# Matmul order in a chunked gated recurrence: two heads in turn, state products after score products

## The chip, the cores and the metric

The kernel runs on one core of one Trainium2 chip. The metric is the device time of one execution in microseconds (us). The kernel before takes 2736.16 us as the median of three runs (2735.38, 2736.16 and 2738.37).

## What is computed

One layer of a hybrid decoder trunk over 2048 tokens of width 1024: a normalised input, one combined input projection, four causal token mixers side by side (A: RG-LRU, B: mLSTM, C: HGRN2, D: GLA), a projection per mixer, a gated merge, an output projection and a final norm. The change lies in the code that C and D share, the gated recurrence:

```python
def gla_chunkwise(q, k, v, log_g):                 # per head, in chunks
    def step(state, xs):
        qc, kc, vc, gc = xs
        G = jnp.cumsum(gc, axis=2)
        diff = jnp.where(mask, G_t - G_s, -jnp.inf)
        A = einsum('bhtd,bhsd,bhtsd->bhts', qc, kc, jnp.exp(diff))          # scores
        o = einsum('bhts,bhse->bhte', A, vc) + einsum('bhtd,bhde->bhte', qc * jnp.exp(G), state)
        state = jnp.exp(G_last) * state + einsum('bhsd,bhse->bhde', kc * jnp.exp(G_last - G), vc)
        return state, o
```

C has four heads with 128 key channels each, D has four heads with 64 key channels and 128 value channels each. Everything is float32.

## The kernel before

The 2048 tokens go through in two halves of 1024. In each half the input projection of most columns comes first (`ahead_pairs`), then `mixers` with the chunked recurrences, then `merge` (branch projections times gates, summed) and `outp`. Large projections take exact splits of their operands into two float32r parts (`proj_ch` L268, `tok_mm` L280, `ip_pair` L422); the recurrences multiply in plain float32, and each such product stands in the trace as two MATMUL records.

`mixers` goes through 12 steps of `gla_tile`, one step for 128 key channels and 512 tokens (4 chunks of 128). Steps 0 to 7 are mixer C: one head fills the 128 partitions, `heads` is `[(0, 128)]`. Steps 8 to 11 are mixer D: two heads share the partitions, `heads` is `[(0, 64), (64, 64)]`, so a product contracts over 64 partitions, those from 0 for one head and those from 64 for the other. There are four such two-head tiles in a half, eight in the program.

One call of `gla_tile` has these stages on TensorE:

- L985, in `diag`: the scores of blocks of 32 tokens on the diagonal, 16 products of 32x32 for a head, once for the inner blocks of 8 and once each for m = 8 and m = 16. A head writes a PSUM bank of its own, block b to partitions from 32 b.
- L1028: the blocks off the diagonal for m = 32 (8 products of 32x32 for a head) and m = 64 (4 products of 64x64 for a head).
- L1050: transposes of the decayed keys. L1056: the chunks' additions to the state, heads in turn. L1063 (VectorE) folds these into the states at the four chunk starts.
- L1071 and L1072: the outputs. L1071 multiplies a chunk's scores (`atv`, 128 partitions) by its values, L1072 the decayed queries (`eg`, the head's partitions alone) by the state, both summed in PSUM.
- L1094: transposes of the normalised outputs; L1095 (VectorE) multiplies them by the gate from the bank.

Six PSUM banks (`bank()`, tiles `mx`) go round among all recurrences; two more (`pb`) belong to the projections. The order on each engine is not written by hand: the framework's scheduler lays the instructions out from priorities and dependencies, and fills the recurrences' waits with projections (L268, L280). During steps 8 to 11 the filler is `merge`'s branch projections, L268. Each engine's instructions stand in that fixed order.

```python
    for c in range(4):
        for b in range(4):
            s0 = c * 128 + b * 32
            T.matmul(ps[b * 32:(b + 1) * 32, c * 32:(c + 1) * 32], wk[p0:p0 + K, s0:s0 + 32],
                     wq[p0:p0 + K, s0:s0 + 32], start=True, stop=True)
```

Of the kernel before, what the change touches and what calls it, by code (L numbers as in the profile page):

```python
# [12 lines left out]
ALU = mybir.AluOpType  # L13
# [4 lines left out]
HT = 1024  # tokens of a half  # L18
DM = 1024
KT = 8  # k tiles of d_model  # L20
U = 516  # columns of one arena unit
NU = 16  # arena units that stay
NA = 4  # tiles of two units that are the arena's outside of the fast products
NY = 8  # the same, and branch outputs in the merge
NP = 6  # merge gates (of 32) computed between the mixers
NE = 5  # of these, so many for the first tokens while the others are split
EPS = 1e-6
NPB = 2  # PSUM banks of the input projection; the other ones are the mixers'
NG = 10  # arena units of the fast products; the other ones are what follows them
PRE = (("mx", 4), ("mo", 4), ("mz", 4), ("hq", 4), ("hz", 4), ("gz", 4), ("gq", 2), ("gk", 2))  # paths to DRAM, with their tiles  # L30
# [12 lines left out]
NORM = {"hz": "hnw", "gz": "gnw"}  # gate paths with the norm's weight in them  # L43
SILU = ("lz", "mz", "hq", "hz", "gz")
FILL = [0, 2, 0, 0, 0, 1, 0, 0, 1, 0, 0, 0, 2, 0]  # merge gates projected before each stage of the mixers

# columns of the packed per-channel vectors
# [10 lines left out]
# channel-major column tiles of the input projection, in the order of wc  # L58
# [10 lines left out]
# constants that depend on shapes alone  # L69
# [29 lines left out]
class Arena:  # L99
    """Units of U columns, handed out in program order, round and round; pairs start at even units."""  # L100
# [47 lines left out]
class Trunk:  # L148
# [107 lines left out]
    def proj_ch(self, pieces, rh, rl, sink, ns=(0, 1)):  # L256
        """128 columns of a product for 512 tokens at a time from weight pieces of 4 k tiles
        each: sink(token slice, PSUM [128, 512])."""
        nc = self.nc
        nk = 4 * len(pieces)  # L260
        for n in ns:
            ts = slice(n * 512, (n + 1) * 512)
            ps = self.pbank()
# [18 lines left out]
    def ip_tok(self, pieces, ncol, evac, single=8):  # L282
        """Token-major column group: evac(first chunk, PSUM [128 tokens, chunks, ncol]); chunks one by one from some."""
# [10 lines left out]
    def ip_tok_k(self, pieces, evac, ks):  # L294
        """The same for 256 columns, k outermost: the operands' tiles are done with one by one."""
        vs = [p[:, 0:256].unsqueeze(1) for p in [self.pbank() for _ in range(NPB)] + [self.bank() for _ in range(8 - NPB)]]
        for k in ks:
            for c in range(8):
                self.tok_mm(vs[c][:, 0, :], c, k, pieces, 256, k == ks[0], k == ks[-1])
        for c in range(8):  # L300
            evac(c, vs[c])

# [6 lines left out]
    def split_first(self, xs):  # L309
        """The normalised input of the first tokens"""  # L310
# [7 lines left out]
    def load_first(self, xs):  # L318
        """The first tokens, and merge gates from them before the norm's factor is known"""
# [40 lines left out]
    def split_blocks(self, xs, st):  # L360
        """The other blocks (two of tokens by two of channels) that the products take: one more as it
        is, four sums; the block left out goes to DRAM."""
# [22 lines left out]
    def restore_block(self):  # L385
        """The block left out of the products, where its sum was."""
# [13 lines left out]
    def ip_pair(self, t0, t1, fin):  # L400
        """Two column tiles of 1024 tokens each; fin of both, [128, 3 free + 1024]."""
# [56 lines left out]
    def ahead_pairs(self):  # L458
        """The projections that the mixers take channel by channel, as far as no other channel or
        earlier token is needed, the RG-LRU, and merge gates: to DRAM."""  # L460
# [122 lines left out]
    def setup_mix(self):  # L583
        nc, c, a, col = self.nc, self.const, self.a, self.col
        V, A = nc.vector, nc.scalar
        # RG-LRU
# [8 lines left out]
        V.tensor_scalar(self.clru, self.clru, 4.0, None, op0=ALU.mult)  # 8 softplus(-lam) / 2  # L595
# [5 lines left out]
        # mLSTM: conv halved (for silu through tanh)  # L601
# [25 lines left out]
        # HGRN2 lower bound: cumulative softmax over the one layer, less its first  # L627
# [14 lines left out]
        # GLA  # L642
        nc.sync.dma_start(self.wlr, a["g_w_lr2"])

# [1 line left out]
    def load_h(self, half, xs, ns=(0, 1)):  # L646
        """The normalised input before it is split: 8 tiles of [128 channels, 1024 tokens]"""
# [41 lines left out]
    def carried(self, f, ci):  # L689
        """The last three tokens before a projection tile, in front of it."""  # L690
# [4 lines left out]
    def load_p(self, name, j, g):  # L695
        """512 tokens of a projection tile"""
# [4 lines left out]
    def conv(self, f, dst, w, b):  # L701
        """w: four per-channel taps, b: bias"""
# [6 lines left out]
    def lru(self, j, fx, zg, temp):  # L709
# [4 lines left out]
        r = [fx[:, h * 512:(h + 1) * 512] for h in range(2)]  # once the convolution is through  # L714
        w = xc
# [39 lines left out]
    def mconv(self, j, f, temp):  # L755
        """silu of the convolution, to DRAM"""
# [10 lines left out]
    def mlstm_rows(self, g, temp):  # L767
        """Gates of 512 tokens: column forms, and row forms in DRAM."""
# [54 lines left out]
    def mlstm(self):  # L823
        """The chunks of 128 tokens; yields where another mixer's work can come in between."""
# [23 lines left out]
        def scores(c, xm, mx, r1b, wib):  # L848
# [10 lines left out]
            # value rows, with a column of ones  # L859
# [681 lines left out]
```

## Time and profile before

| | |
|---|---|
| median of three runs | 2736.16 us (2735.38 to 2738.37) |
| profiled execution, first to last instruction (span) | 2737.5 us |
| time of the profiled execution itself | not listed apart from the span; the runs lie within 2.2 us of it |
| TensorE matmuls (PE) | busy 2603.8 us, 95% of the span, 16800 records |
| TensorE weight loads (PEld) | busy 2153.6 us, 79% |
| VectorE (DVE), ScalarE (ACT), GpSimd (POOL) | busy 1736.1, 1291.6, 1499.7 us |
| mean granted TensorE clock | 0.978 of full |

A record's duration covers its way through the array, and matmuls overlap, so what a matmul costs is read from start to start, not from its duration. The three float32 lines L985, L1028 and L1071/L1072 have small groups on the page; their cost shows in the timeline.

### The profile page before, as it was taken

To read this page: it belongs to the slowest core of one execution; us is meant where nothing else is said; L and a number is where in the kernel's file an instruction comes from. 1 tells how busy PE (TensorE), PEld (TensorE's weight loads), DVE (VectorE), ACT (ScalarE), POOL (GpSimd) and SP (SyncE) were. 2 spreads that over 40 slices of the span, in tenths; PEclk is the share of its full clock that TensorE was granted. 3 is DMA by queue.
4 is the path that set the end of the run, shared out by engine and by line. 5 is a ranking of instruction groups with operands and counts; after the bars stand their busy time and mean duration, and the time that the engine had idled before them with its cause. 6 is when DMAs were issued, how large, how long until landed. Compare 5 with 4: busy or idle time off the path is not lost. (4 is left out here: it accounts for less than half of the span.)

```text
span 2737.5 us, 45829 instructions
## 1 busy us (share of the span) xinstructions
PE 2603.8 (95%) x16800; PEld 2153.6 (79%) x16800; DVE 1736.1 (63%) x2907; ACT 1291.6 (47%) x2763; POOL 1499.7 (55%) x1273
## 2 busy tenths in 40 slices
PE   7889999999989898999999999999999999999999
PEld 5667788877878876778977777888787888777789
DVE  8987853346667767743478878533477677776332
ACT  5554554334444565542465545533344445644433
POOL 5556644444546545567476666444455556554753
PEclk9999999999999999999999999999999999989999
DMA  6132334243454435795442322433335533458821
GB/s 227 61 109 89 101 119 139 98 145 103 148 170 128 121 121 189 253 317 165 155 138 94 110 91 89 139 116 108 135 113 179 167 118 106 146 190 308 273 93 74
DMA packets 227072, 393.03 MB, mean 144 GB/s; under 512 B 20720, under 2 KB 78080, under 8 KB 226848
## 3 DMA queue, kind: packets, MB, share of 16 engines
q1 hardware_dynamic: 226848, 390.11, 42.7%
q8 instruction: 132, 2.16, 0.3%
q14 instruction: 92, 0.75, 0.1%
HBM read 270.42 MB, written 119.60 MB: 142 GB/s over the span
## 5 line engine op out<-in xcount | busy, mean ns | idle before, releaser
L417 POOL TENSOR_TENSOR wl<-wr,wh 128x512 fp32r<-128x512 f32 x264 | 371.6, 1411 | 302.4 <-ACT wh L416 294.4
L417 POOL TENSOR_TENSOR wl<-gth,wh 128x512 fp32r<-128x512 f32 x198 | 284.4, 1437 | 294.6 <-ACT wh L416 284.2
L422 PE MATMUL mx<-s,wh 128*128 128x512 f32 x1296 | 408.5, 395 | 11.3 <-DVE s L306 4.7
L431 DVE TENSOR_TENSOR arena<-arena,mx 128x512 f32<-128x512 f32 x348 | 229.4, 681 | 221.8 <-PE mx L422 208.5
L250 POOL TENSOR_TENSOR wl<-wr,wh 128x512 fp32r<-128x512 f32 (+1 forms) x176 | 250.4, 1431 | 175.4 <-ACT wh L249 139.8
L422 PE MATMUL mx<-hh,wh 128*128 128x512 f32 x760 | 302.0, 397 | 11.9 <-DVE arena L431 10.2
L422 PE MATMUL mx<-hh,wl 128*128 128x512 f32 x760 | 302.3, 398 | 3.1 <-POOL wl L417 3.1
L422 PE MATMUL mx<-hl,wh 128*128 128x512 f32 x760 | 302.0, 397 | 2.0 <-DVE hl L306 2.0
L422 PEld LDWEIGHTS mx<-s,wh 128*128 128x128 f32 x1296 | 243.9, 188 | 70.6 <-DVE s L306 7.1
L268 PE MATMUL pb<-hh,wh 128*128 128x512 f32 x704 | 286.9, 409 | 7.4 <-ACT hh L1284 2.6
L268 PE MATMUL pb<-hl,wh 128*128 128x512 f32 x704 | 286.5, 407 | 5.8 <-DVE hl L1285 5.8
L268 PE MATMUL pb<-hh,wl 128*128 128x512 f32 x704 | 284.3, 404 | 0.0
L416 ACT ACTIVATE wh<-wr 128x512 fp32r<-128x512 f32 x264 | 164.5, 627 | 232.7 <-PE mx L422 98.4
L280 PE MATMUL pb<-wh,hh 128*128 128x256 f32 (+1 forms) x880 | 254.2, 290 | 3.7 <-ACT arena L1006 1.5
L422 PE MATMUL mx<-s,wl 128*128 128x512 f32 x648 | 256.2, 396 | 0.9 <-POOL wl L417 0.9
L280 PE MATMUL pb<-wl,hh 128*128 128x256 f32 (+1 forms) x880 | 253.4, 288 | 1.7 <-POOL wl L250 1.7
L280 PE MATMUL pb<-wh,hl 128*128 128x256 f32 (+1 forms) x880 | 253.5, 288 | 0.0
L416 ACT ACTIVATE wh<-gth 128x512 fp32r<-128x512 f32 x198 | 124.4, 629 | 246.6 <-DVE gth L427 201.6
L249 ACT ACTIVATE wh<-wr 128x512 fp32r<-128x512 f32 (+1 forms) x176 | 110.0, 629 | 161.9 <-PE pb L268 106.6
L422 PEld LDWEIGHTS mx<-hh,wh 128*128 128x128 f32 x760 | 144.3, 190 | 50.1 <-ACT arena L218 11.0
L422 PEld LDWEIGHTS mx<-hh,wl 128*128 128x128 f32 x760 | 143.6, 189 | 41.0 <-POOL wl L417 8.2
L422 PEld LDWEIGHTS mx<-hl,wh 128*128 128x128 f32 x760 | 144.0, 189 | 38.1 <-DVE hl L306 3.2
(614 smaller groups left out, 6177.6 us busy)
## 6 DMA issues: line engine op xcount, KB each, us to landing
wr<-in_wc_dram SPq DMA_DIRECT2D x246, 256.0 KB, 2.7
g<-arena SPq DMA_DIRECT2D x52, 512.0 KB, 3.4
gth<-in_wc_dram SPq DMA_DIRECT2D x66, 256.0 KB, 2.8
wr<-in_wb_dram SPq DMA_DIRECT2D x64, 256.0 KB, 3.0
hl<-y SPq DMA_DIRECT2D x32, 512.0 KB, 5.9
arena<-g SPq DMA_DIRECT2D x48, 256.0 KB, 3.9
arena<-in_xT_dram SPq DMA_DIRECT2D x32, 256.0 KB, 5.1
lw<-g SPq DMA_DIRECT2D x32, 256.0 KB, 3.4
```

What stands on the lines that cost most here:

```text
L249: nc.scalar.activation(hi, raw, AF.Copy)
L250: nc.gpsimd.tensor_tensor(lo, raw, hi, op=ALU.subtract)
L268: nc.tensor.matmul(ps, w[:, ws], h[:, ts], start=(k == 0 and i == 0), stop=(k == nk - 1 and i == 2))
L280: self.nc.tensor.matmul(v, h[:, cs], w[:, ws], start=(first and i == 0), stop=(last and i == 2))
L416: A.activation(hi, w, AF.Copy)
L417: G.tensor_tensor(lo, w, hi, op=ALU.subtract)
L422: nc.tensor.matmul(ps, wp[:, ws], xp, start=(k == 0 and i == 0), stop=(k == 3 and i == 2))
L431: V.tensor_tensor(o, x, y, op=ALU.add)
```

## The change

In `diag` and in the blocks for m = 32 and m = 64, the loop over the heads becomes the innermost one, so the heads' matmuls take turns; the banks of all heads are taken first. In the outputs the products of the scores for all chunks and heads come first, then all products with the state, again with the heads in turn. The first score product of a bank starts it, and the later ones go into it without starting it. With one head the first two loops are what they were. Comments went too, so lines move by a few: L1028 is now L1029, L1050 L1052, L1056 L1058, L1071 L1074, L1072 L1078, L1094 L1100.

```diff
         def diag(wk, wq):
-            for h, (p0, K) in enumerate(heads):
-                ps = self.bank()
-                for c in range(4):
-                    for b in range(4):
-                        s0 = c * 128 + b * 32
+            pss = [self.bank() for _ in heads]
+            for c in range(4):
+                for b in range(4):
+                    s0 = c * 128 + b * 32
+                    for (p0, K), ps in zip(heads, pss):
                         T.matmul(ps[b * 32:(b + 1) * 32, c * 32:(c + 1) * 32], wk[p0:p0 + K, s0:s0 + 32],
                                  wq[p0:p0 + K, s0:s0 + 32], start=True, stop=True)
+            for h, ps in enumerate(pss):
                 yield [t[:, o:o + 128].rearrange("p (c t) -> p c t", t=32) for t, o in ((ad, h * 128), (ps, 0))]
...
-                for h, (p0, K) in enumerate(heads):
-                    ps = self.bank()
-                    for c in range(4):
-                        for b in range(64 // m):
+                pss = [self.bank() for _ in heads]
+                for c in range(4):
+                    for b in range(64 // m):
+                        s0 = b * 2 * m
+                        o = c * 128 + s0
+                        for (p0, K), ps in zip(heads, pss):
                             T.matmul(ps[s0:s0 + m, c * m:(c + 1) * m], w[p0:p0 + K, o:o + m],
                                      w[p0:p0 + K, o + m:o + 2 * m], start=True, stop=True)
+                for h, ps in enumerate(pss):
                     for b in range(64 // m):
...
         pos = [self.bank() for _ in heads]
-        for h, ((p0, K), v, po) in enumerate(zip(heads, vs, pos)):
-            for c in range(4):
-                cc = slice(c * 128, (c + 1) * 128)
-                T.matmul(po[:, cc], atv[:, h, c], v[:, cc], start=True, stop=False)
-                T.matmul(po[:, cc], eg[p0:p0 + K, cc], sts[c][p0:p0 + K, :], start=False, stop=True)
+        for c in range(4):
+            cc = slice(c * 128, (c + 1) * 128)
+            for h, (v, po) in enumerate(zip(vs, pos)):
+                T.matmul(po[:, cc], atv[:, h, c], v[:, cc], start=(c == 0), stop=True, skip_group_check=c > 0)
+        for c in range(4):
+            cc = slice(c * 128, (c + 1) * 128)
+            for (p0, K), po in zip(heads, pos):
+                T.matmul(po[:, cc], eg[p0:p0 + K, cc], sts[c][p0:p0 + K, :], start=False, stop=True, skip_group_check=True)
```

What the scheduler makes of it is seen in the order on TensorE. The first place is the outputs of the third two-head tile of the first half (`mx_100` and `mx_101` are the banks of its two heads). Before:

```order
L1071 MATMUL mx_100<-ma_2_5081,arena 128x128
L1072 MATMUL mx_100<-arena 128x128
L1071 MATMUL mx_100<-ma_2_5081,arena 128x128
L1071 MATMUL mx_101<-ma_3_5082,arena 128x128
L1072 MATMUL mx_101<-arena 128x128
L1071 MATMUL mx_101<-ma_3_5082,arena 128x128
L985 MATMUL mx_104<-ma_1_5080 32x32 x9
```

And now:

```order
L1074 MATMUL mx_100<-ma_2_5081,arena 128x128 x4
L1074 MATMUL mx_101<-ma_3_5082,arena 128x128
L1058 MATMUL mx_99<-ma_2_5081,arena 64x128
...
L1074 MATMUL mx_101<-ma_3_5082,arena 128x128 x3
L1078 MATMUL mx_100<-arena 128x128
L1078 MATMUL mx_101<-arena 128x128
L985 MATMUL mx_104<-ma_1_5080 32x32 x10
```

Score products and state products no longer alternate, and the state products come in pairs of one for each head.

The second place is the blocks for m = 64 of the same tile. Before:

```order
L268 MATMUL pb_98<-hh_66,wl_91 128x512
L1028 MATMUL mx_102<-ma_0_5079 64x64 x4
L1028 MATMUL mx_103<-ma_0_5079 64x64 x4
L1050 MATMUL mx_104<-cst,arena 128x128 x4
L268 MATMUL pb_97<-hh_63,wh_85 128x512
```

And now:

```order
L268 MATMUL pb_97<-hl_74,wh_86 128x512
L1029 MATMUL mx_102<-ma_0_5079 64x64
L1029 MATMUL mx_103<-ma_0_5079 64x64
...
L1052 MATMUL mx_104<-cst,arena 128x128 x4
L268 MATMUL pb_97<-hh_66,wl_92 128x512
```

The heads take turns through all eight products.

The third place is the diagonal blocks that the fourth tile brings first, laid among the third tile's outputs (`mx_104` and `mx_99` are the two heads' banks). They now read:

```order
L1078 MATMUL mx_101<-arena 128x128
L985 MATMUL mx_99<-ma_1_5080 32x32 x16
L1029 MATMUL mx_104<-arena 32x32 x8
L268 MATMUL pb_97<-hl_73,wh_87 128x512
...
L1029 MATMUL mx_99<-arena 32x32 x8
```

Here the scheduler keeps each head's products together, as before: 16 of one head, 16 of the other, and the same in the next blocks.

## Rows read from the trace of the kernel before

**Rows 1.** The page: busy time, share and records of each engine; clock by slices.

```profile
PE 2603.8 (95%) x16800; PEld 2153.6 (79%) x16800; DVE 1736.1 (63%) x2907; ACT 1291.6 (47%) x2763; POOL 1499.7 (55%) x1273
PEclk9999999999999999999999999999999999989999
```

**Rows 2.** Windows: length, busy us (records) by engine, PEclk, DMA share, GB/s.

```profile
780.00:1050.00 270.00, 245.56 (x2526) 220.90 (x2524) 194.90 (x476) 144.08 (x441) 148.72 (x160) 0.96 0.42 128
1050.00:1200.00 150.00, 142.86 (x1557) 109.84 (x1557) 96.20 (x172) 68.55 (x187) 69.51 (x71) 0.95 0.72 247
...
2395.00:2545.00 150.00, 143.15 (x1565) 111.10 (x1564) 98.89 (x174) 70.96 (x197) 71.42 (x73) 0.95 0.72 253
```

**Rows 3.** Waits of PE from 1050 to 1200 us: total us, times, longest.

```profile
PE pb L268 <- DVE hl L1285: 2.7, 3, 1.6
PE mx L985 <- DVE ma L1095: 2.7, 1, 2.7
...
PE mx L985 <- DVE mb L1095: 0.6, 1, 0.6
```

**Rows 4.** PE timeline, outputs of a one-head tile: start us, us, instruction, records.

```profile
812.66 0.39 PE L1072 MATMUL mx<-arena,mb 128*128 128x128 f32 x2
812.88 0.39 PE L1071 MATMUL mx<-mb,arena 128*128 128x128 f32 x2
813.11 0.39 PE L1072 MATMUL mx<-arena,mb 128*128 128x128 f32 x2
```

**Rows 5.** PE timeline, outputs of the third two-head tile of the first half.

```profile
1148.17 0.49 PE L1071 MATMUL mx<-ma,arena 128*128 128x128 f32 x2
1148.59 0.48 PE L1072 MATMUL mx<-arena 64*128 64x128 f32 x2
1149.00 0.71 PE L1071 MATMUL mx<-ma,arena 128*128 128x128 f32 x4
1149.64 0.49 PE L1072 MATMUL mx<-arena 64*128 64x128 f32 x2
...
1150.47 0.37 PE L985 MATMUL mx<-ma 64*32 64x32 f32 x18
1150.78 0.49 PE L1072 MATMUL mx<-arena 64*128 64x128 f32 x2
...
1152.44 0.49 PE L1072 MATMUL mx<-arena 64*128 64x128 f32 x4
1152.87 0.49 PE L1071 MATMUL mx<-ma,arena 128*128 128x128 f32 x2
...
1154.53 0.61 PE L985 MATMUL mx<-ma 64*32 64x32 f32 x46
```

**Rows 6.** PE timeline, score blocks of two-head tiles among projections.

```profile
1139.98 0.96 PE L1028 MATMUL mx<-ma 64*64 64x64 f32 x16
1140.88 0.66 PE L1050 MATMUL mx<-cst,arena 128*128 128x128 f32 x4
...
1167.26 0.40 PE L268 MATMUL pb<-hl,wh 128*128 128x512 f32 x1
1167.49 0.40 PE L268 MATMUL pb<-hh,wl 128*128 128x512 f32 x1
1167.82 0.76 PE L985 MATMUL mx<-arena 64*32 64x32 f32 x64
1168.50 0.51 PE L268 MATMUL pb<-hh,wh 128*128 128x512 f32 x1
```

**Rows 7.** Groups by line and form: L1072 with 64 partitions, records, busy us, mean ns.

```profile
L1072 PE MATMUL mx<-arena 64*128 64x128 f32 x96 | 20.4, 323 | 0.0
...
L1072 PE MATMUL mx<-arena,ma 64*128 64x128 f32 x32 | 6.8, 323 | 0.0
```

**Rows 8.** Windows: the stretch where the DMA engines are busiest.

```profile
1145.00:1185.00 40.00, 40.00 (x418) 31.23 (x417) 22.79 (x45) 20.07 (x53) 20.36 (x19) 1.00 0.96 331
```

**Rows 9.** Waits of the SP queue, 1050 to 1200 us: loads of weight pieces.

```profile
SPq L248 <- POOL wl L250: 7.8, 8, 2.5
```

More of the change, by code (lines that the diff above doesn't have):

```diff
@@ L1021, in gla_tile @@
             else:
-                for h, (p0, K) in enumerate(heads):
-                    ps = self.bank()
-                    for c in range(4):
-                        for b in range(64 // m):
-                            s0 = b * 2 * m
-                            o = c * 128 + s0
+                pss = [self.bank() for _ in heads]
[4 more added lines that the diff above has]
+                        for (p0, K), ps in zip(heads, pss):
                             T.matmul(ps[s0:s0 + m, c * m:(c + 1) * m], w[p0:p0 + K, o:o + m],
                                      w[p0:p0 + K, o + m:o + 2 * m], start=True, stop=True)
+                for h, ps in enumerate(pss):
                     for b in range(64 // m):
```

## Prediction

> **What bounds the kernel now.** The page comes first: TensorE's matmuls are busy for 95% of the span and no other engine for more than 63% [rows 1]. The windows then show where the two-head tiles run, from about 1050 to 1200 us and again from 2395 to 2545 us. There PE is busy for 142.86 and 143.15 of 150 us, while in the one-head steps before, 780 to 1050 us, it is idle for 24 of 270 us [rows 2]. The waits say why the two-head stretch is so full: only 2.7 us go to a branch's split (L1285) and 3.3 us to banks that L1095 still reads [rows 3]. Projections L268 fill every gap, so TensorE time that the recurrence gives back is taken by projections that would otherwise run later, in `merge`. The rest of `merge` has no other cover and gets shorter by as much. A microsecond of PE time saved in the two-head tiles is therefore worth about one at the end.
>
> **What a product costs is read from start to start.** In a one-head tile L1071 and L1072 alternate too, and each product (two records) starts 0.22 us after the one before: 812.66, 812.88, 813.11 [rows 4]. In a two-head tile the same 128 columns take 0.42 us: 1148.17, 1148.59, 1149.00 [rows 5]. The two kinds differ in one thing: with two heads L1071 contracts over 128 partitions and L1072 over 64 [rows 5, 7]. Where two L1071 follow each other in the two-head tile (x4 at 1149.00) they take 0.64 us, that is 0.42 for the first and 0.22 for the second. So it is the change between 128 and 64 partitions that costs some 0.2 us a product, in both directions. One row more decides the size of the gain: the x4 of L1072 at 1152.44 are two state products, one for each head, which the scheduler happened to put side by side. The next instruction starts at 1152.87, 0.43 us later, as after a single one. Two heads side by side cost the time of one.
>
> **Outputs.** The tile shown runs from 1148.17 to 1154.53, less 0.31 us of foreign L985 work (1150.47 to 1150.78): 6.05 us [rows 5]. By the built order the other seven alternate in the same way, seven groups of L1072 each; eight tiles make 48.4 us. After the change the eight score products of a tile follow each other: 8 x 0.22 = 1.78 us and 0.2 us for the changes before and behind, 1.98 us. The state products stand in pairs, but not all in one piece. The built order has three tiles with groups of one, two and one pairs and five with one and three, with projections or diagonal blocks between. A group costs 0.42 us for its first pair and 0.22 for each further one: 0.42 + 0.64 + 0.42 = 1.48 us in three tiles, 0.42 + 0.86 = 1.28 us in five. Sum: 8 x 1.98 + 3 x 1.48 + 5 x 1.28 = 26.7 us. The outputs save 48.4 - 26.7 = 21.7 us. I take 21, since in some tiles L268 or L1056 already stood where I counted an L1071.
>
> **Scores within blocks.** The 16 records of m = 64 take 0.90 us (1139.98 to 1140.88) and the 64 of a diagonal block 0.68 us (1167.82 to 1168.50) [rows 6]. Going in from a projection costs 0.1 us of it: the last L268 lasts 0.33 us to the next start instead of 0.23 [rows 6]. For alternating heads in these blocks there is no row of its own, so I bound it. At least nothing is gained: 0 us. At most all of it halves, as with the state products: 24 diagonal blocks at 0.68, 8 for m = 64 at 0.90 and 8 for m = 32, priced at half a diagonal block (0.34), since they have half its records. That is 26.2 us, halved 13 us. For m = 64 I take a gain of a third, 0.3 us, because what lies at the two ends of a block does not overlap. Six of the eight blocks alternate in the built order: 1.8 us. A diagonal block's records already start 0.68 / 64 = 0.0106 us apart, since its four places in the bank overlap; I take 0.1 us each for the 16 of 24 that alternate at least in part, 1.6 us, and 0.6 us for m = 32. Together 4 us, much nearer to nothing than to half.
>
> The Trainium skill ("TensorE: Matmul & The Clock Gate", section "Wait — 56ns, not 53.3ns?") states that starts never come closer than about 25 ns, however small the product. By that the alternation of 32-column blocks could give nothing, and by the page this term would be the 1.8 us of m = 64 alone. The row contradicts it, 10.6 ns a record [rows 6], and the measurement decides; the rule gets no chance of its own.
>
> **What is added.** No instruction is added or removed, no transfer either. Counted over the whole order, changes of partitions or columns outside the 64-partition state products rise from 336 to 344; at 0.1 us each, as going in from L268, 0.8 us are lost. The first head's mask waits for both heads' products now, under 0.7 us later; the second head's comes no later than before, and L268 fills PE meanwhile. The one-head tiles keep their products at 0.22 us, as scores and states both contract over 128 there [rows 4]: nothing.
>
> **The sum.** 21 + 4 - 0.8 = 24 us of PE time. The order says where it goes: between the first diagonal product of the two-head steps and the last L1094 stand 364 L268 before and 406 now in the first half, 358 and 402 in the second. These 86 at 0.23 us [rows 6] are 20 us of projections drawn forward, so the recurrence stays about as long and the rest of `merge` shortens. I take 2 us off for waits that a faster PE newly meets: 22 us. The profiled span of 2737.5 us becomes 2715.5; it stands 1.3 us above the median of the runs, so the time forecast is **2714 us**, 0.8% less. Its own range is 2704 us (scores near their upper bound) to 2720.
>
> **Rivals.** *The heads do not overlap*, the change does less than it says: the pair at 1152.44 is one kind of instance, eight in the program. Then 32 pairs cost 0.22 us more each, 7 us, and the 4 us of the blocks go: 24 - 11 - 2 = 11 us saved, 2725 us. Against it speaks the row itself [rows 5].
>
> *The feed becomes the bound.* From 1145 to 1185 us the DMA engines are busy to 0.96 at 331 GB/s [rows 8], and the change draws L268 forward into this stretch, with their weights and gates. If the third and fourth tile gave nothing back in either half, half the gain would be left: 2725 us. Against it: PE is busy for all 40 of these 40 us [rows 8], and the weight loads wait for a free buffer, not the other way round (L248 behind L250, 7.8 us) [rows 9].
>
> *The recurrence's own chain is the bound*, as between 780 and 1050 us, where PE idles 9% [rows 2]: then the PE time saved becomes idle time, 2736 us. Against it: 4.7% idle in the two-head stretch, and the fill above.
>
> *Slower: the banks.* Alternating heads need two banks free before the block can go on, where one was enough, and PE stands still for both, with all L268 queued behind. Such a wait exists now: L985 behind L1095, once 2.7 us and once 0.6 [rows 3]. The place is 40 blocks (five in each of eight tiles). At 0.55 us a block it eats the 22 us; beyond 0.7 us the kernel is slower by over 0.2%; at 0.9 us it adds 36 us and the time is 2750 us. The Trainium skill ("TensorEngine Tiling (Array Packing)", Gotcha 1: PSUM Pressure) warns of just this, since row tiles write different banks. Against it: before, too, a block took two of the six banks in the round, and the waits on banks are 3.3 us in the whole stretch [rows 3].
>
> **How the numbers follow.** Forecast 0.70, no overlap 0.08, feed 0.12, chain 0.06, banks 0.04. The range from 2704 to 2728 us takes in the forecast with the bound of the scores and both half gains, some 0.87 of the chance, less what a shifted order may do elsewhere. A measurement can tell about 0.2% (5.5 us) from no change: faster 0.90, same 0.06, slower 0.04.
>
> **What would show it.** Right: in the timeline L1074 in rows of up to 16 records 0.11 us apart and L1078 as x4, x8 or x12 with 0.22 us for each further four; both lines near 27 us from start to start instead of 47; L1029 with 64x64 near 0.6 us a block; PE idle time in the two-head stretch still near 7 us; the steps after 1200 us earlier by about 11 us. Wrong: L1078 of two heads 0.22 us apart; new waits of L985 or L1029 on L1095; L268 waiting for L250; more time at half clock. The clock is 0.95 in the two-head stretch [rows 2], so a few more microseconds there at the lower level, 1.2 of 2.4 GHz, would cost about half of themselves.

## The result, and the profile after

The changed kernel takes 2759.73 us (median of four runs, 2750.28 to 2761.32) beside 2735.77 us for the kernel before (four runs). The ratio is 1.0074, with a 95% interval of 1.0057 to 1.0092: slower by 0.7%, where 0.8% faster was forecast. The profiled execution took 2760.07 us with a span of 2758.3 us, 20.8 us more than before.

The page of the changed kernel, line of the engines, and its windows over the two-head stretches:

```profile
PE 2589.9 (94%) x16800; PEld 2141.9 (78%) x16800; DVE 1729.8 (63%) x2907; ACT 1302.3 (47%) x2771; POOL 1498.9 (54%) x1273
```

```profile
1050.00:1200.00 150.00, 132.94 (x1565) 104.21 (x1564) 95.09 (x173) 69.33 (x180) 68.25 (x72) 0.93 0.71 240
1200.00:1400.00 200.00, 189.55 (x1189) 169.54 (x1188) 85.84 (x117) 86.52 (x193) 125.16 (x104) 0.98 0.52 173
2395.00:2545.00 150.00, 129.69 (x1479) 101.16 (x1469) 103.13 (x183) 73.02 (x189) 73.99 (x75) 0.91 0.70 236
```

PE's busy time fell by 13.9 us. But its idle time (span less busy) rose from 133.7 to 168.4 us, and that is where the loss is: in each two-head stretch PE is now idle for 17 and 20 of 150 us, where it was idle for 7 [rows 2]. ScalarE shows eight instructions more, all of them table loads.

**The matmuls do what was forecast.** PE's timeline of the changed kernel, outputs of the second two-head tile and a block for m = 64 (start us, us, instruction, records):

```profile
1105.32 2.05 PE L1074 MATMUL mx<-mb,arena 128*128 128x128 f32 x16
1107.31 0.49 PE L1078 MATMUL mx<-arena,ma 64*128 64x128 f32 x4
1107.73 0.50 PE L268 MATMUL pb<-hh,wh 128*128 128x512 f32 x1
...
1108.62 0.94 PE L1078 MATMUL mx<-arena,ma 64*128 64x128 f32 x12
1109.49 0.50 PE L268 MATMUL pb<-hh,wh 128*128 128x512 f32 x1
...
1144.48 0.68 PE L1029 MATMUL mx<-ma 64*64 64x64 f32 x16
1145.10 0.66 PE L1052 MATMUL mx<-cst,arena 128*128 128x128 f32 x4
```

Eight score products take 1.99 us (1.98 forecast), a group of one state pair 0.42 us and one of three 0.87 us (0.42 and 0.86 forecast), the block for m = 64 0.62 us where it took 0.90 [rows 6].

**PE waits where it did not wait before.** The waits of PE over the whole span (us in total, times, longest):

```profile
PE mx L1100 <- ACT arena L1096: 18.6, 5, 6.0
PE pb L268 <- DVE gth L1317: 16.1, 3, 7.2
...
PE mx L985 <- DVE arena L1009: 9.3, 4, 3.7
```

L1100 is the transpose of the normalised outputs (L1094 before), and waits for the norm on ScalarE, L1096. L268 waits for a projection bank, which L1317 on VectorE reads out. Six gaps carry most of it: 7.06 and 7.19 us ahead of L268 (one in each half), 3.55 and 3.59 us ahead of L1100 in the third two-head tile, 6.04 and 5.24 us in the fourth. Together 32.7 us, beside 34.7 us of added idle time. The kernel before has no wait for the norm in any two-head tile (1.8 us once, in a one-head tile).

**The 7 us ahead of L268.** VectorE's timeline up to L1317, then PE's:

```profile
1126.23 1.23 DVE L1291 TENSOR_TENSOR hl<-hl,hh 128x1024 fp32r<-128x1024 f32 x1 [3.08 <-ACT hh L1290]
...
1129.36 1.23 DVE L1291 TENSOR_TENSOR hl<-hl,hh 128x1024 fp32r<-128x1024 f32 x1
1130.50 1.22 DVE L962 TENSOR_TENSOR_SCAN ma<-cst,ma 128x512 f32<-128x512 f32 x1
1131.63 1.42 DVE L1008 TENSOR_TENSOR ma<-ma,ma 128x256 f32<-128x256 f32 x1
...
1133.31 2.35 DVE L1291 TENSOR_TENSOR hl<-hl,hh 128x1024 fp32r<-128x1024 f32 x2
1135.58 0.41 DVE L1008 TENSOR_TENSOR arena<-arena 128x256 f32<-128x256 f32 x1
1136.03 0.69 DVE L1317 SCALAR_TENSOR_TENSOR gth<-gth,pb 128x512 f32<-128x512 f32 x1
```

```profile
1136.77 0.80 PE L268 MATMUL pb<-hh,wh 128*128 128x512 f32 x1 [7.06 <-DVE gth L1317]
1137.37 0.63 PE L268 MATMUL pb<-hl,wh 128*128 128x512 f32 x1
1137.79 0.63 PE L268 MATMUL pb<-hh,wl 128*128 128x512 f32 x1
```

L1291 is the VectorE half of a branch's split (L1290 the ScalarE half), work of `merge` that the scheduler now issues earlier. Four of them, a microsecond and more each, stand with the recurrence's own work ahead of the instruction that frees PE's bank. In the kernel before the same four came one at a time, between read-outs of banks:

```profile
1140.21 0.68 DVE L1311 SCALAR_TENSOR_TENSOR gth<-gth,pb 128x512 f32<-128x512 f32 x1
1140.81 1.22 DVE L1285 TENSOR_TENSOR hl<-hl,hh 128x1024 fp32r<-128x1024 f32 x1
...
1143.92 0.67 DVE L1311 SCALAR_TENSOR_TENSOR gth<-gth,pb 128x512 f32<-128x512 f32 x1
1144.52 1.46 DVE L1285 TENSOR_TENSOR hl<-hl,hh 128x1024 fp32r<-128x1024 f32 x1
```

**The waits for the norm.** ScalarE in the third tile of the changed kernel, and PE behind it:

```profile
1152.99 1.28 ACT L1307 ACT_TABLE_LOAD   x1
1154.28 0.63 ACT L1307 ACTIVATE ma<-ma 128x512 f32<-128x512 f32 x1
...
1157.86 1.28 ACT L227 ACT_TABLE_LOAD   x1
1159.15 0.30 ACT L227 ACTIVATE ssq<-ssq,small 128x4 f32<-128x4 f32 x1
1159.47 1.28 ACT L1044 ACT_TABLE_LOAD   x1
...
1161.93 1.28 ACT L227 ACT_TABLE_LOAD   x1
...
1163.54 1.28 ACT L1090 ACT_TABLE_LOAD   x1
...
1165.56 1.64 ACT L1096 ACTIVATE arena<-mx,ssq 128x128 f32<-128x128 f32 x6
```

```profile
1162.01 0.40 PE L268 MATMUL pb<-hh,wl 128*128 128x512 f32 x1
1165.96 0.47 PE L1100 MATMUL mx<-cst,arena 128*128 128x128 f32 x1 [3.55 <-ACT arena L1096]
```

L1307 is the Tanh of a merge gate, drawn forward too. It now runs ahead of the norm and, with an ACT_TABLE_LOAD of 1.28 us, replaces the table that holds logarithm and exponential together (the kernel loads that one by name behind the mixers' own Tanhs). From there each change between Ln (L227) and Exp (L1044, L1090) loads a table: four loads, 5.1 us, between the squares and L1096. Before, both Ln and the first Exp of the third tile came ahead of the first Tanh, and its norm needed no load:

```profile
1157.13 0.33 ACT L227 ACTIVATE ssq<-ssq,small 128x4 f32<-128x4 f32 x1
1157.32 0.24 ACT L1084 ACTIVATE ssq<-ssq 128x4 f32<-128x4 f32 x1
1157.58 1.28 ACT L1301 ACT_TABLE_LOAD   x1
```

A load alone makes no wait. The fourth tile's norm had two of them before the change as well, and PE did not wait, since the order left it 24 L268 (5.9 us) between the tile's last state product and its transposes:

```profile
1196.83 1.28 ACT L227 ACT_TABLE_LOAD   x1
1198.62 1.28 ACT L1084 ACT_TABLE_LOAD   x1
```

In the changed kernel's third tile 23 L268 (7.0 us) stand there, and the norm takes 10.3 us from the first square.

In the fourth tile of the changed kernel ScalarE stood on a Tanh whose gate was still being loaded. The state products ended at 1198.8 us; the squares (L1088) began more than 5 us later, and PE's transposes had to wait:

```profile
1203.61 0.63 ACT L1307 ACTIVATE arena<-arena 128x512 f32<-128x512 f32 x1 [5.86 <-DMA arena<-g]
1204.14 0.26 ACT L1088 ACTIVATE arena<-mx 128x128 f32<-128x128 f32 x1
```

```profile
1214.10 1.25 PE L1100 MATMUL mx<-cst,arena 128*128 128x128 f32 x4 [6.04 <-ACT arena L1096]
```

**The clock adds to it.** The windows of the changed kernel behind the 7 us gap (PEclk is the third number from the end):

```profile
1137.00:1141.50 4.50, 4.50 (x11) 3.53 (x12) 1.45 (x6) 0.83 (x2) 0.78 (x2) 0.50 1.00 346
1142.00:1160.00 18.00, 18.00 (x196) 14.46 (x195) 9.38 (x20) 10.38 (x28) 7.00 (x8) 1.00 0.84 304
```

After the idle time the granted clock is 0.50, 1.2 GHz, and L268 starts every 0.43 us instead of every 0.23.

Theory, then: the products are as cheap as forecast, but the projections that were drawn forward bring `merge`'s Tanhs and splits with them, and these stand ahead of the norm and of the banks' read-out in the in-order queues of ScalarE and VectorE (the in-order theory, called Theory Q in the first expectations). Rivals: alternating heads or the new bank use do harm of themselves (H); drawing projections forward is itself too much for the loads (L; in the first expectations L stands for any new order costing some 20 us).

### The profile page after: what moved, and what is told of

Read it like the earlier page. It is cut to its first block, busy times and chain, and to the rows that moved or that the text cites. A ratio compares the mean times of both kernels' runs of the same rounds, so it can differ in the third digit from the quotient of the medians.

```text
span 2758.3 us, 45797 instructions
## 1 busy us (share of the span) xinstructions
PE 2589.9 (94%) x16800; PEld 2141.9 (78%) x16800; DVE 1729.8 (63%) x2907; ACT 1302.3 (47%) x2771; POOL 1498.9 (54%) x1273
## 4 chain that ended last, share of the span: by engine, by line
PE 43%; DVE 7%; ACT 4%; DMA 4%; issue 2%; POOL 2%; SPq 0%; POOLq 0%; ACTq 0%; DVEq 0%
PE mx L422 15%; PE pb L268 12%; PE pb L280 5%; PE pb L422 5%; PE mx L280 1%; POOL wl L417 1%; DVE hl L1291 1%; PE mx L1074 1%; PE mx L985 1%; DVE arena L680 1%; DVE arena L431 1%; DMA arena<-rdram 1%; DVE arena L706 1%; PE mx L1078 0%; PE mx L1100 0%
## 5 line engine op out<-in xcount | busy, mean ns | idle before, releaser
L422 PE MATMUL mx<-s,wh 128*128 128x512 f32 x1296 | 412.6, 398 | 13.3 <-DVE gv L625 4.9
L268 PE MATMUL pb<-hh,wh 128*128 128x512 f32 x704 | 291.8, 416 | 23.8 <-DVE gth L1317 16.1
L422 PE MATMUL mx<-hh,wh 128*128 128x512 f32 x760 | 302.6, 398 | 9.0 <-DVE arena L431 8.6
L422 PE MATMUL mx<-hh,wl 128*128 128x512 f32 x760 | 303.1, 399 | 4.1 <-POOL wl L417 4.1
L422 PEld LDWEIGHTS mx<-s,wh 128*128 128x128 f32 x1296 | 246.4, 190 | 74.0 <-DVE s L306 5.5
L422 PE MATMUL mx<-hl,wh 128*128 128x512 f32 x760 | 302.3, 398 | 1.4 <-DVE hl L306 1.4
L268 PE MATMUL pb<-hl,wh 128*128 128x512 f32 x704 | 289.1, 411 | 4.9 <-DVE hl L1291 4.4
L268 PE MATMUL pb<-hh,wl 128*128 128x512 f32 x704 | 287.5, 409 | 0.0
L422 PE MATMUL mx<-s,wl 128*128 128x512 f32 x648 | 258.2, 399 | 2.0 <-POOL wl L417 2.0
L280 PE MATMUL pb<-wh,hh 128*128 128x256 f32 (+1 forms) x880 | 254.6, 290 | 4.8 <-DVE lrt L1123 4.1
L280 PE MATMUL pb<-wl,hh 128*128 128x256 f32 (+1 forms) x880 | 253.6, 288 | 1.3 <-POOL wl L250 1.3
L280 PE MATMUL pb<-wh,hl 128*128 128x256 f32 (+1 forms) x880 | 254.8, 290 | 0.0
L268 PEld LDWEIGHTS pb<-hh,wh 128*128 128x128 f32 x704 | 137.9, 196 | 58.9 <-DVE gth L1317 16.4
L422 PEld LDWEIGHTS mx<-hh,wh 128*128 128x128 f32 x760 | 144.6, 190 | 47.4 <-ACT arena L218 9.4
L422 PEld LDWEIGHTS mx<-hh,wl 128*128 128x128 f32 x760 | 144.0, 190 | 42.8 <-POOL wl L417 9.7
```

The source lines that it names most:

```text
L268: nc.tensor.matmul(ps, w[:, ws], h[:, ts], start=(k == 0 and i == 0), stop=(k == nk - 1 and i == 2))
L280: self.nc.tensor.matmul(v, h[:, cs], w[:, ws], start=(first and i == 0), stop=(last and i == 2))
L422: nc.tensor.matmul(ps, wp[:, ws], xp, start=(k == 0 and i == 0), stop=(k == 3 and i == 2))
```

## The experiments

All ratios are against runs of the kernel before on the same chip; they differ by up to 0.14% from quotients of the medians. A hold is an ordering constraint on ScalarE's queue alone: it changes no computation, but the scheduler lays out the whole program anew around it, so no run below differs from its parent in one instruction only. The number of projections drawn forward changes too: between the first diagonal product of the two-head tiles and their last transpose, both halves together, the change has 86 more L268 than the kernel before, e3 69, e4 46, e5 44, e6 25, e10 9 and e11 47.

| run | edit | median, us | ratio, 95% interval | span, PE busy, PE idle |
|---|---|---|---|---|
| (after) | | 2759.73 | 1.0074, 1.0057 to 1.0092 | 2758.3, 2589.9, 168.4 |
| e1_outs_only | outputs alone | 2738.13 | 1.0004, 0.9988 to 1.0020 | 2734.5, 2586.5, 148.0 |
| e2_heads_only | score blocks alone | 2744.75 | 1.0023, 1.0005 to 1.0041 | 2748.4, 2606.8, 141.6 |
| e3_hold_norm | Tanhs and last splits behind the norm | 2751.25 | 1.0052, 1.0031 to 1.0073 | 2749.3, 2589.1, 160.2 |
| e4_hold_both | e3 and e5 together | 2727.93 | 0.9962, 0.9944 to 0.9980 | 2726.8, 2582.6, 144.2 |
| e5_hold_split | third branch's splits spread | 2735.83 | 0.9992, 0.9977 to 1.0006 | 2731.9, 2592.0, 139.9 |
| e6_no_log | no logarithm in the norm | 2725.77 | 0.9962, 0.9948 to 0.9977 | 2724.5, 2583.1, 141.4 |
| e7_hold_both_9 | e4, Tanhs held earlier | 2731.81 | 0.9986, 0.9966 to 1.0006 | 2726.1, 2582.1, 144.0 |
| e8_outs_hold_both | e1 with both holds | 2725.61 | 0.9968, 0.9949 to 0.9988 | 2729.7, 2592.3, 137.4 |
| e9_before_holds | before with both holds | 2746.73 | 1.0021, 1.0005 to 1.0038 | 2746.7, 2603.1, 143.6 |
| e10_join | one Ln and Exp for both heads | 2733.35 | 0.9983, 0.9964 to 1.0001 | 2740.9, 2595.2, 145.7 |
| e11_join_both | e4 and e10 together | 2727.91 | 0.9967, 0.9952 to 0.9982 | 2719.2, 2580.7, 138.5 |
| e12_before_join | before with one Ln and Exp | 2748.27 | 1.0027, 1.0010 to 1.0044 | 2744.7, 2604.3, 140.4 |

The runs of one kernel scatter by up to 0.8% here (before: 2728.35 to 2747.00 in the first group), so a profiled span can lie some microseconds off its kernel's median.

**One part at a time.** e1 keeps the change's outputs and has the score blocks as before; e2 the other way round.

```diff
 e1
-            pss = [self.bank() for _ in heads]
+            for h, (p0, K) in enumerate(heads):
+                ps = self.bank()
...
 e2
-        for c in range(4):
-            cc = slice(c * 128, (c + 1) * 128)
-            for h, (v, po) in enumerate(zip(vs, pos)):
+        for h, ((p0, K), v, po) in enumerate(zip(heads, vs, pos)):
+            for c in range(4):
```

> Only the outputs are changed; the heads do not take turns in the score blocks. Theory Q (queues: merge work that the scheduler draws forward stands in ScalarE's and VectorE's order ahead of the recurrence, and TensorE waits behind it): the state products still come in pairs, PE saves 21 us, and in the built order the norm's Ln and Exp stand together in the first half (3 table loads in the overlap with the merge) but not in the second (7, as in the changed kernel); so waits of about 17 us in the second half alone, 2728 to 2736 us. Theory H (the alternation of heads in the score blocks, two banks at a time, is what costs): 2715 us, as the alternation is gone.

> Only the heads take turns; the outputs are as before. Theory Q: PE saves 4 us; the built order has 5 table loads in each half where the kernel before has 3 and the changed one 7, and a Tanh between a norm's Ln and Exp, so about half of the changed kernel's new waits, 2740 to 2748 us. Theory H: the whole loss, 2755 us or more.

e1 came out at no change, just above what was expected of the in-order theory and 23 us above what H gave; e2 where the in-order theory had it, though its mechanism was not what that theory named: the waits for the norm in the two-head tiles come to 2.9 us only, beside 3.3 us for a projection bank and 3.6 us of the score blocks (L1029) for VectorE. Neither half of the change reaches the loss of the whole. e1 holds a comparison within one run. In its first half both norms of the third tile are through before the first Tanh, and the transposes hardly wait. In its second half the Tanh comes first and the four loads between Ln and Exp are there. The halves also differ in what is drawn forward, 5 L268 fewer than before the change in the first and 49 more in the second, so the comparison does not separate the order from the amount. PE's waits in e1 from 1120 to 1220 us and from 2480 to 2590 us:

```profile
PE mx L1097 <- ACT arena L1093: 0.9, 2, 0.5
```

```profile
PE mx L1097 <- ACT arena L1093: 7.8, 2, 7.1
```

**The queues.** e3 keeps the gates' Tanhs behind the third tile's norm, the twelfth and later ones and the last branch's splits behind the fourth's. e5 spreads the third branch's splits alone, e4 does both.

```diff
 e3
-                        A.activation(t[:, :512], t[:, :512], AF.Tanh, scale=0.5)
+                        i = A.activation(t[:, :512], t[:, :512], AF.Tanh, scale=0.5)
+                        self.after(i, self.lm[2]['exp'])
+                        if ni * 16 + j * 2 + h >= 32 + 11:
+                            self.after(i, self.lm[3]['exp'])
 e3, splits of branch ni = 3 (behind an instruction of the fourth tile)
+                return [self.lm[3]['norm']]
 e5, splits j = 1 to 3 of branch ni = 2 (behind three instructions of the third and fourth tile)
+                return [(self.lm[2]['dg'], self.lm[3]['wk'], self.lm[3]['w', 8])[j - 1]]
```

> The changed kernel with an order on ScalarE alone: the merge gates' Tanh may not come before the third two-head tile's norm, the twelfth and later ones not before the fourth's, and the last branch's splits not before the fourth tile's scaling, as in the kernel before. No matmul is moved by hand. Theory Q: 29 or so table loads instead of 37, the waits of L1100 on L1096 (3.6 and 6.0 us in the first half, 3.6 and 5.2 in the second) go, 2738 to 2745 us. Theory H: 2760 us as before. Theory L (any new order costs some 20 us, whatever it is): no relation to the held work, 2750 to 2770 us.

> The change, with the third branch's splits alone tied to later places on ScalarE (the norms stay where the scheduler puts them). In-order theory: the two 7 us waits of L268 behind the freeing of its bank go, as in e4; the waits for L1096 behind the table loads stay in part (the static order has 5 loads in each overlap instead of 7). If the two holds add up, e4 less e3 is worth 23 us and this run is 2733 to 2742 us; if the split is the only cause and the norm a bystander, it comes out as e4, 2724 to 2732; if the splits are no cause, 2752 to 2762. Load theory (the drawn-forward projections are short of weights and gates, whoever stands first): 2750 to 2765.

> The same, and the splits of the third branch are spread as in the kernel before: one behind the third tile's block copies, one behind the fourth tile's first keys, one behind its m = 8 weights. Theory Q: the waits of L268 on L1317 (7.1 us in the first half, 7.2 in the second) go too, 2722 to 2732 us. Theory H: 2760 us. Theory L: 2750 to 2770 us.

e4 turned a loss of 0.74% into a gain of 0.38% with the change's matmul code untouched. H, and L as any new order, which both expected 2750 us and more of it, fall. L as too much drawn forward does not fall with e4, which draws 46 L268 forward instead of 86. The parts add up: from the change's 1.0074, e3 takes 0.0022 and e5 0.0082, together 0.0104; e4 takes 0.0112. But e3's interval overlaps the change's, so its own share is not shown. e3 was 6 us above its expected range, and inside that of L. Its waits from 1120 to 1220 us and from 2480 to 2590 us say why: the third tile's wait is gone, the wait for the bank stayed as it was, and at the fourth tile the Tanhs' waits for their gates still stand ahead of the squares (6.28 and 2.06 us in the second half).

```profile
PE pb L268 <- DVE gth L1330: 7.0, 1, 7.0
PE mx L1103 <- ACT arena L1099: 4.8, 1, 4.8
```

```profile
PE mx L1103 <- ACT arena L1099: 9.1, 1, 9.1
PE pb L268 <- DVE gth L1330: 6.9, 1, 6.9
```

In e5 one split instead of four stands ahead of the bank's read-out on VectorE, and the wait for the bank is 3.9 us in the first half; from 2480 to 2590 us there is none. The first half:

```profile
PE mx L1103 <- ACT arena L1099: 5.4, 2, 3.3
PE pb L268 <- DVE gth L1327: 3.9, 1, 3.9
```

e5's new order also has two table loads less in each overlap than the change, so its 24 us are not the splits' alone. In e4 3.9 us of the wait for the bank stay in the first half and none in the second; the third tile's waits for the norm are 0.3 us at most, the fourth's 3.9 and 6.4 us.

**The table loads.** e6 leaves the logarithm out of the norm of mixers C and D and takes the exponential of the scaled variance itself, so it computes another norm factor and is of use for its time alone. e10 keeps the computation and gives both heads one Ln and one Exp; e11 adds it to e4.

```diff
 e6
-            self.ln(ss, ss, scale=1.0 / 128, bias=eps)
+            V.tensor_scalar(ss, ss, 1.0 / 128, eps, op0=ALU.mult, op1=ALU.add)
             A.activation(ss, ss, AF.Exp, scale=-0.5)
...
 e10, e11: squares of both heads first
+                A.activation(o[:, cc], po[:, cc], AF.Square, accum_out=ss[:, h * 4 + c:h * 4 + c + 1])
+        self.ln(ss, ss, scale=1.0 / 128, bias=eps)
+        A.activation(ss, ss, AF.Exp, scale=-0.5)
+        for h, (po, o, zg) in enumerate(zip(pos, os_, zgs)):
```

> The change with the logarithm in the norm of mixers C and D left out: VectorE makes the scaled variance and ScalarE exp(-0.5 x) of it, so the factor is another one; all other work is the same. Tanh and exp are in one table, so the alternation Ln, Exp in the merge overlap costs no table loads (one in each overlap instead of seven). In-order theory with tables: the waits of L1100 at the third tile (3.6 us in each half) go and those at the fourth shrink by 2 to 3 us each; the 7 us waits of L268 and the Tanh's waits for loads stay: 2743 to 2752 us. If table loads are no part of it: 2756 to 2764. Load theory: 2756 to 2764 as well.

> The change with one Ln and one Exp for the two heads of a tile (squares of both heads first, into one tile of eight columns), nothing held. No Tanh can get between two logarithms, so the merge overlap has 3 table loads instead of 7, as before the change. In-order theory with table loads: the waits of L1100 at the third tile go and the run comes near e6, 2724 to 2736 us, if the splits of the third branch do not stand together ahead of L1317; with them there, 7 us waits of L268 in each half stay and it is 2738 to 2748. If the logarithm's own work and not the alternation was what e6 took away: 2750 to 2762.

> e4 with one Ln and one Exp for the two heads. In e4 a Tanh between the two Ln of the second half's fourth tile cost two table loads (2.56 us) ahead of a 6.4 us wait. In-order theory: that wait falls to about 4 us and the rest is as in e4: 2722 to 2728 us. Without that theory, as e4: 2726 to 2731.

e6 gained 17 us more than expected. The waits for the norm went (1.8 us are left in the two-head tiles), but the 7 us for the bank, which I thought independent of it, went as well (0.4 us are left): the scheduler put the splits elsewhere. Waits of L1029 for VectorE came in their place, 7.9 us in the first half and 4.4 us in the second. So e6 shows that removing the alternation is enough to lose the waits, but not how much of the gain is the loads' own. e10, which keeps the logarithm, has 0.8 us of waits for the norm in the two-head tiles (and 3.1 us in the last one-head tile) and 3.3 us for the banks that L1317's successor reads; L1029 waits 3.8 and 4.7 us for VectorE. Its ten executions lie 18 us apart, and its median is inside the range expected for that case. It also draws only 9 L268 forward, so it does not separate the loads from the amount either.

e11's waits for the norm are small (0.3 us from 1120 to 1220, 1.5 us from 2480 to 2590 us), with a wait of 3.9 us of the score blocks for VectorE beside them. It draws as many L268 forward as e4, and PE is as full in the two-head stretches as before [rows 2]. Its profiled execution is the shortest of all:

```profile
1050.00:1200.00 150.00, 141.51 (x1610) 111.01 (x1609) 101.80 (x180) 75.10 (x205) 84.15 (x81) 0.97 0.79 272
2395.00:2545.00 150.00, 143.87 (x1624) 112.30 (x1624) 99.01 (x181) 77.77 (x208) 90.77 (x82) 0.98 0.82 282
```

That execution is also the fastest of its seven (2720.99 us; the others take 2727.38 to 2731.82). By its median e11 is as fast as e4 and no faster, which both expectations allow for, so it decides nothing between them.

**Better holds.** e7 puts two more Tanhs behind the fourth tile's norm; e8 is e1 with both holds.

```diff
 e7
-                        if ni * 16 + j * 2 + h >= 32 + 11:
+                        if ni * 16 + j * 2 + h >= 32 + 9:
```

> As e4, but the tenth and later gate Tanhs (instead of the twelfth and later) stand behind the fourth tile's norm on ScalarE, so that its squares wait for fewer gate loads. In-order theory: the wait of L1100 at the fourth tile (3.9 us and 6.4 us in e4) falls to 1 to 3 us, if nothing else is late: 2720 to 2727 us. If the gates' sums then come late and L268 waits for its bank instead, 2727 to 2735. Load theory: as e4, 2726 to 2730.

> Only the outputs changed (score blocks as before), with both holds. The score blocks were priced at 4 us of the gain. Matmul prices and in-order theory: some 4 us behind e4 if it has no wait that e4 has not, 2727 to 2735 us, and below outputs alone (2738) by what its own waits of 2 to 7 us come to. If the alternation of the score blocks does harm of its own, it is faster than e4: 2715 to 2725 us. If the holds do nothing for it: 2736 to 2740.

e7 did not do what it was for: its waits at the fourth tile are 3.47 and 7.49 us, e4's 3.91 and 6.43. A Tanh still stood between the two Ln in the second half. Its median lies 5 us above the range that went with shorter waits, and its interval takes in no change. e8 is as fast as e4, and at 2725.6 us between its two ranges: PE is busy for 9.7 us more, 2.9 of them in the old score blocks, and idle for 6.8 us less. Both beat the kernel before and the changed one, by some 10 and 33 us. That e8 and e4 come out alike, on two chips and with intervals of 0.2% to either side, fits the score blocks' part of the change being worth no more here than the waits that come with it; a small harm of the alternation itself is not ruled out.

**Controls on the old order of the matmuls.** e9 is the kernel before with e4's holds, e12 the kernel before with e10's edit.

> Control: the kernel before (old order of the matmuls) with both holds of e4. The kernel before has hardly any wait for its norm (1.8 us) and its third branch's splits are spread already, so the in-order theory expects nothing for it: 2730 to 2742 us beside a before of about 2737. The gain of e4 would then be the matmul order's. If the holds themselves make the program faster, whatever the matmul order, it comes out near e4 or e8: 2722 to 2729 us.

> Control in the other direction: the kernel before (old matmul order) with one Ln and one Exp for two heads. Its order draws 412 and 382 L268 into the overlap (364 and 358 before), so projections go forward with the old matmuls too; its third tile has a Tanh ahead of Ln and another ahead of Exp, so 5 loads in each overlap instead of 3. In-order theory: waits for the norm of 2 to 4 us at the third tile, 2738 to 2748 us. If the matmul order is what makes the difference between two kernels and ScalarE's order is not: within 2734 to 2739, as before.

Neither gains; both lose 0.2 to 0.3%, e9 5 us more than expected (its longest new waits are 4.2 us of L1031, the score blocks, for VectorE and 3.5 us of L268 for its bank). The gain of e4 is thus not the holds' own. e12 comes out at the upper end of what was expected (0.3 us above it), but not for the reason given: its waits for the norm in the two-head tiles are 0.4 us at most, although its third tile has three loads around the norm, and its longest new wait is 4.9 us of L268 for a bank. In that tile of the first half 38 L268 (10.8 us) stand between the last state product and the transposes. Loads on ScalarE cost PE nothing here while the order leaves it projections to run.

## Why the prediction was wrong

Summed over all matmul records, from start to next start and less the idle time before the next, and with the page's idle time:

| us | before | forecast | after | e11 |
|---|---|---|---|---|
| outputs, all tiles | 76.8 | -21 | 57.0 (-19.7) | 58.1 (-18.7) |
| score blocks over 64 partitions | 32.8 | -4 | 27.7 (-5.1) | 27.9 (-4.9) |
| projections L268, L280, L422 | 2216.7 | 0 | 2230.1 (+13.4) | 2216.7 (0.0) |
| other matmuls | 277.3 | +0.8 | 274.8 (-2.6) | 277.7 (+0.4) |
| PE idle | 133.7 | +2 | 168.4 (+34.7) | 138.5 (+4.8) |

- **Bound by PE in the two-head stretch: right for the kernel before, as far as is shown.** In e11's profiled execution, with most of the waits gone, the span is 18.3 us shorter for 23.1 us less PE time. But that is its fastest execution; by the medians e11 is 10 us faster than the kernel before, and e4 too. So by the medians less than half of those 23 us reach the end, and that a microsecond saved is worth about one is not shown.
- **Outputs, 21 us, and scores, 4 us: right**, to 1.3 and 1.1 us. Within the scores m = 64 gave 2.9 us (1.8 forecast), m = 32 0.7 (0.6) and the diagonal blocks 1.5 (1.6). But the diagonal blocks take 17.9 and 18.0 us in e8 and e1 too, with the old order, so their 1.5 us are not the alternation's; there the forecast hit a number by luck and not its cause. That 128 and 64 partitions in turn cost 0.2 us a product, and that two state products of two heads cost the time of one, held.
- **"These 86 at 0.23 us are 20 us of projections drawn forward, so the recurrence stays about as long": this step failed.** I counted PE's side of the drawn-forward work and nothing else. A projection of `merge` needs its gate's Tanh and its branch's split on ScalarE and VectorE, and the order on those two engines was there to be read as well as PE's. It shows the Tanh ahead of both Ln of the third tile, and the splits of a branch together. From the first diagonal product of the two-head tiles to their last transpose the recurrence took 168.3 and 164.1 us, where it had taken 148.9 and 146.4. A second thing was left out: the outputs of both heads now end together, so the third tile's first square starts when the last state product has ended (1155.67 us), where it had started 1.2 us ahead of that (1153.39); the prediction counted such a delay for the masks of the score blocks alone.
- **"I take 2 us off for waits that a faster PE newly meets": missed by 33 us**, and by the 13.4 us that projections took longer; 7.6 us of these are 40 L268 at the lower clock right behind the six waits. The clock was named at the end of the prediction, as a remark, and had no term.
- **The rivals.** Alternating heads do overlap. For banks that L1101 (L1095 before) reads, PE waits once, 0.7 us; the rival on the slower side was the wrong mechanism. PE does wait for a bank, but one of the projections', behind the splits. The feed has a part: the Tanh's 5.86 us for a gate's load is what the fourth tile stands on. e4 draws 20 and 26 L268 more into the two overlaps than the kernel before, and e11 15 and 32, and both gain, so drawing some forward is not what costs; that 42 and 44 of them cost nothing by their number is not shown. The recurrence's chain became the bound at four places, the norms of the third and fourth tiles, through what stood ahead of them in ScalarE's queue. Of the signs of being wrong that the prediction listed, only the time at half clock came.

What stays open: how the 24 us of e5 divide between splits, table loads and the rest of the order, since each hold moved all three and the number of projections drawn forward; and why e9 and e12 lose 0.2 to 0.3%, which is nearly as much as e4 gains. No run puts the joint table back in behind the gate's Tanh and leaves the rest, so the loads' own part was not measured.

## What to carry to other kernels

When a change makes one engine faster and the scheduler fills the time with other work, follow that work's operations onto every engine it touches, in the built order, and see what they now stand ahead of in an in-order queue, and how much work the order leaves the fast engine behind which to hide it. Here one Tanh of 0.6 us in front of a norm brought four table loads with it, because it separated functions that shared a table. Once the matmul order is right, hold the filler's side work behind the latency-critical chain: here two constraints, with the new layout that they led to, made the difference between 0.7% slower and 0.4% faster.

## What the runs showed of the hardware

- A change between Ln and Exp behind a Tanh costs 1.28 us of load, and the neighbours follow within 0.02 us (the Ln starts at 1159.15, 1.29 us after its load; the next load at 1159.47, 0.02 us after its end). The Trainium skill ("ScalarE: Activation LUTs", section "What ACT_TABLE_LOAD costs") gives about 1283 ns for the load, which the trace confirms, and a drain of about 1380 ns on top, which it does not show: by that page's 2.66 us a switch (an estimate) the four loads of the third tile would take 10.6 us, and they took 5.1.
- The waits of 3.5 to 7 us cost more than themselves: behind the six of them 40 L268 go at 0.42 to 0.43 us a start instead of 0.23, 7.6 us more. In the whole changed kernel 77 L268 go at that pace, 41 in the kernel before; shorter waits have it behind them too (1.86 us at 1057.33). The Trainium skill ("TensorE: Matmul & The Clock Gate", Part 1) has two levels, 1.2 and 2.4 GHz; the trace agrees, with 0.50 and 1.00 granted in the windows above.
- Alternating heads are worth less in short products. The state products of two heads cost less than half when paired (23.3 us before, 10.9 after, both over 64 partitions; fewer changes between 128 and 64 partitions have a part in it), the 64x64 products a third less (8.4 and 5.5 us, six of eight blocks alternating), the 32x32 products of the diagonal nothing that these runs can tell from the old order.
